# A hybrid decoder trunk on one core: the key norm by GpSimd powers, the triangular solve with every fourth column to a partition, and a beginning with x from ScalarE's queue

## The chip, the cores and the metric

The kernel runs on one core of a Trainium2 chip. The metric is the device time of one execution in microseconds, the median over runs. One core has TensorE (PE, matmuls and transposes), VectorE (DVE), ScalarE (ACT), GpSimd (POOL) and SyncE (SP, which issues DMAs here), each with an instruction queue of its own, and 16 DMA engines behind them.

## The reference

Two layers over 256 tokens of width 1024. Each layer has an FFN, a mixer of three branches (latent attention, gated linear attention, RWKV-7), cross-attention into 256 memory tokens and a second FFN, each between two RMS norms. All weights and results are float32.

```python
for l in range(DEPTH):                      # DEPTH = 2
    ng = norm_g[l]
    x = x + 0.5 * _rmsnorm(_swiglu(_rmsnorm(x, ng[0]), w_ffn_in[l, 0], w_ffn_out[l, 0]), ng[1])
    y = _mixer_block(_rmsnorm(x, ng[2]), ...)
    x = x + _rmsnorm(y, ng[3])
    y = _mem_attn(_rmsnorm(x, ng[4]), _rmsnorm(mem, mem_norm[l]), ...)
    x = x + _rmsnorm(y, ng[5])
    x = x + 0.5 * _rmsnorm(_swiglu(_rmsnorm(x, ng[6]), w_ffn_in[l, 1], w_ffn_out[l, 1]), ng[7])
```

The part of the RWKV branch that the change touches (8 heads of 64):

```python
kk = heads(k * k_k).astype(jnp.float32)
kk = kk / jnp.maximum(jnp.linalg.norm(kk, axis=-1, keepdims=True), 1e-12)
...
def step(state, inp):
    r_t, w_t, k_t, v_t, kk_t, a_t = inp
    sa = jnp.einsum('bhij,bhj->bhi', state, kk_t)
    state = (state * w_t[:, :, None, :] - sa[..., None] * (kk_t * a_t)[:, :, None, :]
             + v_t[..., None] * k_t[:, :, None, :])
    return state, jnp.einsum('bhij,bhj->bhi', state, r_t)
```

## The kernel before

**Order.** The kernel's body is recorded first, as a list of instructions with their tiles, and a list scheduler (class Program) gives each engine its order. It works out which instructions depend on which from the memory that they touch (`footprint`), estimates each one's duration (`cost`), knows that GpSimd and VectorE may share a port (`shared`), and simulates the queues (`forward`) in several passes. All instructions are issued from one line, L403, which is why every row of the profile names that line. Nothing is reordered later: each engine works through its list and waits at each instruction for what it needs. DMAs use eight completion semaphores in turn, in the order of issue, and each DMA waits until the one eight before it has landed.

**Products.** Activations and weights are split into two fp32r parts. `wload` brings a weight chunk into one of three raw buffers (raw0 to raw2); ScalarE casts it to `whi`, VectorE subtracts to `wlo`, and `mm3` makes three matmuls of each pair. Results are collected in the PSUM banks b_g0 and b_g1; transposes go through b_s0 and b_s1, and the branches use b_ya and b_yb. Most other data live in `heap` (float32) and `heapr` (fp32r), which the profile shows under one name each.

**Beginning.** While `fine` is set, the first FFN's weights come in pieces. x comes in four DMAs of 128x512 on SyncE's queue, the gain norm_g in two DMAs that broadcast 1024 values to 128 partitions. VectorE multiplies x by the gain, PE transposes the product into b_s, ScalarE casts it into heapr and VectorE subtracts for the low part. The mean square is applied behind the product.

**Key norm** (`rwkv_keys`). sv holds the squares of the keys, features on partitions. Four matmuls with `selh` sum them per head into 8 rows of 256 tokens (b_ya); VectorE takes a maximum into `rn`, ScalarE the square root, VectorE the reciprocal, and four matmuls with `wd` broadcast `rn` back to the 64 features of each head. VectorE then multiplies.

**Solve** (`rwkv_solve`, once for each layer and half of the tokens, four in all; t = 0 is called the first here, t = 1 the second). The recurrence over chunks of 32 tokens becomes the inverse of unit lower triangular 32x32 matrices. Of each matrix 4 partitions share the 32 columns, 8 each. VectorE does 31 steps of two instructions, multiply and subtract, on 128 x (31−j) x 8 elements. The result goes through DRAM twice, into `si` and `sx`, and is read back in other layouts as X1 and XT. In `rwkv_back` PE multiplies 32x32 blocks with X1; these are the `32x32` matmuls of the profile.

Of the kernel before, what the change touches and what calls it, by code (L numbers as in the profile page):

```python
# [24 lines left out]
D = 1024  # L25
# [23 lines left out]
class Program:  # L49
# [20 lines left out]
    def footprint(self, ap):  # L70
        t = ap.tensor
        if "PSUM" in str(ap.space):
            return [((ap.name, 0, 0), (1, 1))]
        if "DRAM" in str(ap.space):
            return [((ap.name, 0, 0), (1, 1))]
        key = (ap.name, ap.offset, ap.ap)
        f = self.prints.get(key)
        if f is None:
# [56 lines left out]
    def cost(self, op):  # L135
# [76 lines left out]
    def order(self):  # L212
# [10 lines left out]
        self.size = [o[2][0].nbytes() / self.DMA_RATE if o[0].name == "sync" else 0.0 for o in ops]  # L223
# [16 lines left out]
        for i, users in enumerate(self.users):  # L240
            t = self.at[i]
            for b in users:
                b.start, b.end = min(b.start, t[0]), max(b.end, t[1] + (4.0 if self.eng[i] == "sync" else 0.2))
        return order

    def lag(self, i, s):
        if self.eng[i] == "sync":
            return self.DMA_START + self.size[i] + self.DMA_END
        return self.LAT[self.eng[i]][self.eng[i] != self.eng[s]]
# [36 lines left out]
    def forward(self, rank):  # L286
# [15 lines left out]
        while len(order) < n:  # L302
# [9 lines left out]
            if e == "gpsimd" and t < held["vector"]:  # L312
                free[e] = held["vector"] + 0.03
                continue
# [3 lines left out]
            i = heapq.heappop(ready[e])[1]  # L318
            if e == "scalar" and self.table(ops[i]) not in (None, table):
# [58 lines left out]
            if e == "sync":  # L378
                dma_free = max(dma_free, t + self.DMA_START) + self.size[i]
                end = dma_free + self.DMA_END  # L380
                done.append(end)
            for s in self.succ[i]:
                rt[s] = max(rt[s], end if e == "sync" else end + self.LAT[e][e != eng[s]])
# [81 lines left out]
class Trunk:  # L465
# [184 lines left out]
    def constants(self):  # L650
# [38 lines left out]
        selh = self.tile("selh", [128, 134], F32)  # L689
        g.memset(selh, 0.0)  # L690
        g.memset(selh[0:64, 102:103], 1.0)
        g.memset(selh[64:128, 103:104], 1.0)
        self.selh = [selh[:, 6 - 2 * hp:134 - 2 * hp] for hp in range(4)]
        self.two = selh[:, 102:104]
# [12 lines left out]
        sel(e4.rearrange("p (a b) -> p a b", b=8), [[1, 32], [-1, 8]], 0, -8, op=ALU.is_equal)  # L707
# [37 lines left out]
        self.rn = self.tile("rn", [128, 256], F32)  # L745
        g.memset(self.rn, 0.0)
# [82 lines left out]
    def gain(self, src):  # L829
        b = self.h.alloc(D)  # L830
        for c in self.halves if self.fine else [slice(0, D)]:
            self.nc.sync.dma_start(b[:, c], src[c].partition_broadcast(128))
        return b

# [45 lines left out]
    def ffn(self, l, i, st, post_g, nxt, after_first=None):  # L880
        hb, lb, xh, xl = st["xp"]
        rs = st["rs"]
        wi = self.kview(self.w["w_ffn_in"][l, i])
# [7 lines left out]
        def inn(c):  # L891
# [14 lines left out]
            def view(k0, kn):  # L906
                return [(0, wi[:, k0:k0 + kn, c * 256:c * 256 + 256]), (256, wi[:, k0:k0 + kn, FF + c * 256:FF + c * 256 + 256])]
# [112 lines left out]
    def rwkv_keys(self, l):  # L1020
# [26 lines left out]
        for q in range(2):  # L1047
            pb = self.bank("ya", (2, 256))
            for j in range(2):
                hp = 2 * q + j  # L1050
                self.mm(pb[:, j, :], self.wd[:, hp * 128:hp * 128 + 128], self.rn)
                self.stt(kv[:, hp, :], k0[:, hp, :], self.col(l, 14 + hp), pb[:, j, :], MULT, MULT)
        for hp in range(4):
# [106 lines left out]
    def rwkv_solve(self, l, t):  # L1160
# [45 lines left out]
    def rwkv_back(self, l, t):  # L1206
# [9 lines left out]
        x1, hh = X1.v("p (h n) -> p h n", h=8), HH.v("p (h n) -> p h n", h=8)  # L1216
# [12 lines left out]
        h.free(X1, HH, LN)  # L1229
# [539 lines left out]
    def run(self):  # L1769
# [33 lines left out]
        nxt, st = into(0, 0)  # L1803
        self.fine = True
        for t in range(2):
            for c in self.halves:
                nc.sync.dma_start(self.x[:, t, c], w["x"][0, t * 128:t * 128 + 128, c])
        nxt(None)
        nxt(0)
        nxt(1)  # L1810
# [47 lines left out]
```

## Time and profile before

| | |
|---|---|
| median of 3 runs | 1641.55 us (1638.19 to 1644.56) |
| profiled execution | 1642.84 us, span 1641.1 us |
| mean granted TensorE clock | 0.99 |
| busy share of the span | PE 97%, VectorE 67%, ScalarE 59%, GpSimd 7% |
| bytes moved by DMA | 274.90 MB, mean 168 GB/s |

The table comes from the times and the page of the profiled execution. A row of the timeline gives start, length, engine, line, operation, tile written <- tiles read, shapes, count and, in brackets, the idle time ahead of it with what ended it. A row of the groups ends in busy time, mean ns of one, and idle time. A row of the chain of waits has start and length. A row of the DMA issues ends in the KB of one and the median us from issue to landing. A window's row has the busy time of each engine, then PE's granted clock, the share of the DMA engines and GB/s.

### The profile page before, as it was taken

The numbers are of one execution on the slowest core, as the hardware profiler recorded it, in microseconds if no ns is written. First come the engines' busy times: TensorE is split into PE (matmuls) and PEld (weight loads), VectorE is DVE, ScalarE is ACT, GpSimd is POOL, SyncE is SP. The second block draws the span as 40 slices with busy tenths as digits, with TensorE's granted clock in tenths as the row PEclk, the third lists the DMA queues.
The fourth block names the chain that finished last, engine by engine and source line by source line (L and its number), as shares of the span: only waits on it lengthen the run. The fifth ranks groups of instructions, "written<-read, shape, count | busy, mean of one in ns | idle before, by whom it ended". The sixth has DMA issues, their size and how long they took to land.

```text
span 1641.1 us, 23827 instructions
## 1 busy us (share of the span) xinstructions
PE 1591.3 (97%) x8623; PEld 1330.6 (81%) x8623; DVE 1102.5 (67%) x2110; ACT 967.3 (59%) x1889; POOL 113.2 (7%) x207
## 2 busy tenths in 40 slices
PE   7999999999999999999999999999999999999998
PEld 5788888877878987888878887987877889878886
DVE  5555668869967566555575556579699675675555
ACT  5455576769545556545565455858775565565554
POOL 7000010000200101000010001100002110010000
PEclk9999999999999999999999999999999999999999
DMA  7656543532656545555545555435337555354652
GB/s 247 224 167 203 164 153 96 173 91 92 229 159 199 193 142 166 201 197 188 196 158 193 192 185 156 142 97 167 98 98 229 181 184 188 114 189 160 207 178 103
DMA packets 206090, 274.90 MB, mean 168 GB/s; under 512 B 28148, under 2 KB 157650, under 8 KB 205972
## 3 DMA queue, kind: packets, MB, share of 16 engines
q1 hardware_dynamic: 205972, 273.39, 50.9%
q8 instruction: 67, 1.10, 0.3%
q14 instruction: 51, 0.42, 0.1%
HBM read 270.60 MB, written 2.75 MB: 167 GB/s over the span
## 4 chain that ended last, share of the span: by engine, by line
PE 79%; DVE 10%; ACT 5%; DMA 3%; issue 2%; SPq 0%; DVEq 0%; POOLq 0%; ACTq 0%; POOL 0%
PE b_g L403 42%; PE b_ya L403 15%; PE b_s L403 11%; PE b_yb L403 10%; DVE heap L403 5%; DVE wlo L403 3%; ACT heap L403 3%; DMA raw<-in_w_ffn_in_dram 1%; ACT whi L403 1%; DMA raw<-in_w_ffn_out_dram 1%; ACT L403 1%; DVE heapr L403 1%; DVE small L403 1%; DVE x L403 1%; DMA si<-heap 0%
## 5 line engine op out<-in xcount | busy, mean ns | idle before, releaser
L403 DVE TENSOR_TENSOR wlo<-raw,whi 128x512 fp32r<-128x512 f32 (+1 forms) x964 | 648.7, 688 | 382.7 <-ACT whi L403 370.8
L403 ACT CAST whi<-raw 128x512 fp32r<-128x512 f32 (+1 forms) x964 | 582.8, 620 | 457.1 <-PE b_g L403 218.3
L403 PE MATMUL b_g<-whi,heapr 128*128 128x512 f32 (+2 forms) x1904 | 651.7, 402 | 8.8 <-ACT heapr L403 6.0
L403 PEld LDWEIGHTS b_g<-whi,heapr 128*128 128x128 f32 x1904 | 356.9, 190 | 89.4 <-ACT heapr L403 10.2
L403 PE MATMUL b_g<-wlo,heapr 128*128 128x512 f32 (+2 forms) x952 | 365.3, 398 | 3.1 <-DVE wlo L403 3.1
L403 PEld LDWEIGHTS b_g<-wlo,heapr 128*128 128x128 f32 x952 | 180.6, 190 | 40.4 <-DVE wlo L403 5.9
L403 PE MATMUL b_g<-heapr,whi 128*128 128x256 f32 x1104 | 200.3, 291 | 1.7 <-DVE heap L403 1.5
L403 PE MATMUL b_ya<-whi,heapr 128*128 128x512 f32 x480 | 177.9, 394 | 0.3 <-ACT heapr L403 0.3
L403 PE MATMUL b_yb<-whi,heapr 128*128 128x512 f32 x480 | 175.6, 393 | 0.0
L403 PE MATMUL b_s<-whi,heapr 128*128 128x512 f32 x448 | 174.9, 399 | 0.0
L403 PEld LDWEIGHTS b_g<-heapr,whi 128*128 128x128 f32 x1104 | 165.0, 193 | 6.4 <-DVE heap L403 2.9
L403 DVE TENSOR_TENSOR heap<-heap 128x256 f32<-128x256 f32 (+29 forms) x376 | 130.9, 364 | 11.3 <-ACT heap L403 5.9
L403 PE MATMUL b_g<-heapr,wlo 128*128 128x256 f32 x552 | 131.8, 287 | 0.0
L403 POOL TENSOR_SCALAR small<-small 128x1 f32<-128x1 f32 (+2 forms) x52 | 34.3, 659 | 1276.2 <-ACT heap L403 1109.7
L403 PE MATMUL b_s<-ident,heap 128*128 128x128 f32 (+2 forms) x449 | 92.7, 276 | 13.0 <-DVE heap L403 10.4
L403 PEld LDWEIGHTS b_yb<-whi,heapr 128*128 128x128 f32 x480 | 89.8, 188 | 18.8 <-DVE heapr L403 0.2
L403 PEld LDWEIGHTS b_ya<-whi,heapr 128*128 128x128 f32 x480 | 89.3, 188 | 19.2 <-ACT heapr L403 0.5
L403 DVE TENSOR_TENSOR heapr<-b_s,heapr 128x256 fp32r<-128x256 f32 (+2 forms) x148 | 75.3, 510 | 37.6 <-ACT heapr L403 37.1
L403 ACT CAST heapr<-b_s 128x256 fp32r<-128x256 f32 (+2 forms) x148 | 65.4, 443 | 58.1 <-PE b_s L403 50.7
L403 PEld LDWEIGHTS b_s<-whi,heapr 128*128 128x128 f32 x448 | 83.6, 188 | 18.2 <-DVE heap L403 0.6
L403 PEld LDWEIGHTS b_g<-heapr,wlo 128*128 128x128 f32 x552 | 94.9, 192 | 0.6
L403 PE MATMUL b_ya<-wlo,heapr 128*128 128x512 f32 x240 | 92.9, 392 | 0.0
(161 smaller groups left out, 1540.7 us busy)
## 6 DMA issues: line engine op xcount, KB each, us to landing
raw<-in_w_ffn_in_dram SPq DMA_DIRECT2D x172, 512.0 KB, 4.9
raw<-in_w_in_dram SPq DMA_DIRECT2D x50, 1024.0 KB, 5.0
raw<-in_w_ffn_out_dram SPq DMA_DIRECT2D x44, 1024.0 KB, 6.9
raw<-in_mem_wkv_dram SPq DMA_DIRECT2D x16, 1024.0 KB, 5.4
raw<-in_w_branch_dram SPq DMA_DIRECT2D x12, 1024.0 KB, 5.4
raw<-in_w_out_dram SPq DMA_DIRECT2D x8, 1024.0 KB, 5.0
raw<-in_mem_wq_dram SPq DMA_DIRECT2D x8, 1024.0 KB, 5.2
raw<-in_mem_wo_dram SPq DMA_DIRECT2D x8, 1024.0 KB
```

Source lines behind the costliest of these rows:

```text
L403: getattr(eng.real, method)(*a, **k)
```

## The change

Five parts, all in one file:

1. *The scheduler.* A DMA issued by any engine is treated as one (before: only SyncE's). Inputs in DRAM make no dependencies, and other DRAM tensors make them by pieces of 32 elements. The rule for the port that VectorE and GpSimd share counts fewer GpSimd instructions. The whole order is planned anew.
2. *Weight loads.* While `fine` is set, the two halves of a piece of w_ffn_in come in one DMA: 8 of 128x2x256 stand where 16 of 128x256 stood.
3. *Key norm.* Eight matmuls of two columns give the sums with tokens on partitions (128 x 2 x 8); VectorE takes the maximum into `nz`, GpSimd raises it to the power −0.5, PE transposes `nz` twice, and ScalarE copies the result to the heap as rn. The broadcast matmuls stay. No Sqrt is left on ScalarE.
4. *Solve.* A partition holds every fourth column of its matrix. At step j only j//4 + 1 of the 8 columns are not zero yet, and only these are worked on. sx is written by four DMAs instead of one, and two ScalarE copies (XN) reorder X1 ahead of the 32x32 matmuls that read it.
5. *Beginning.* x and the gain come on ScalarE's queue, the gain as 8 rows of 128, which PE transposes to a column per block. x is transposed as it is, and VectorE multiplies by the gain while it reads PSUM.

Cut to what the prediction speaks of:

```diff
@@ cost, shared, forward
+        if method == "dma_start":
+            return 0.47
...
-        ins = [x for x in ins if int(np.prod(x.shape[1:])) > 1]
-        return len(ins) >= (2 if eng.name == "vector" else 1) or eng.name == "gpsimd"
+        if eng.name == "gpsimd":
+            return any(x is not k.get("scalar1", a[2] if len(a) > 2 else None) for x in ins)
+        return sum(int(np.prod(x.shape[1:])) > 1 for x in ins) > 1
@@ rwkv_keys
-        for hp in range(4):
-            self.mm(ps[:, 0:256], self.selh[hp], sv[:, hp, :], hp == 0, hp == 3)
-        rn = self.rn[96:104, :]
-        nc.vector.tensor_scalar(rn, ps[96:104, 0:256], 1e-24, None, MAX)
-        self.act(rn, rn, AF.Sqrt)
-        nc.vector.reciprocal(rn, rn)
+        for t in range(2):
+            for hp in range(4):
+                o = t * 8 + 2 * hp
+                self.mm(ps[:, o:o + 2], sv[:, hp, t * 128:t * 128 + 128], self.two)
+        nz = self.nz[:, :, 96:104]
+        nc.vector.tensor_scalar(nz, ps[:, 0:16].rearrange("p (t n) -> p t n", t=2), 1e-24, None, MAX)
+        nc.gpsimd.tensor_tensor(nz, nz, self.mhalf[:, 0:1].unsqueeze(1).to_broadcast([128, 2, 8]), ALU.pow)
+        pt = self.bank("ya")[:, 0:256]
+        for t in range(2):
+            self.tr(pt[:, t * 128:t * 128 + 128], self.nz[:, t, :])
+        rn = h.alloc(256)
+        nc.scalar.copy(rn.ap, pt)
@@ rwkv_solve
-            n = 31 - j
-            self.tt(tm[:, 0:n, :], xlv[:, j + 1:32, j:j + 1].to_broadcast([128, n, 8]),
-                    xx[:, j:j + 1, :].to_broadcast([128, n, 8]), MULT, eng)
-            self.tt(xx[:, j + 1:32, :], xx[:, j + 1:32, :], tm[:, 0:n, :], SUB, eng)
+            n, m = 31 - j, j // 4 + 1
+            self.tt(tm[:, 0:n, 0:m], xlv[:, j + 1:32, j:j + 1].to_broadcast([128, n, m]),
+                    xx[:, j:j + 1, 0:m].to_broadcast([128, n, m]), MULT, eng)
+            self.tt(xx[:, j + 1:32, 0:m], xx[:, j + 1:32, 0:m], tm[:, 0:n, 0:m], SUB, eng)
...
-        nc.sync.dma_start(sx, TM.ap)
+        sxw = sx.rearrange("(b a) (c x i) -> x b (a c) i", a=4, c=2, x=4)
+        for x in range(4):
+            nc.sync.dma_start(sxw[x], TM.v("p (c i) -> p c i", c=8)[x:128:4])
@@ rwkv_back
+        XN = h.alloc(256)
+        for b in (0, 64):
+            nc.scalar.copy(XN.v("p (h c x) -> p h c x", h=8, x=4)[b:b + 32], X1.v("p (h x c) -> p h c x", h=8, x=4)[b:b + 32])
@@ run, and new functions
+    def first_gain(self, src):
+        nc = self.nc
+        row, g = self.h.alloc(128), self.sm.alloc(8)
+        nc.scalar.dma_start(row[0:8, :], src.rearrange("(k c) -> k c", c=128))
+        ps = self.bank("ya")[:, 0:8]
+        self.tr(ps, row[0:8, :])
+        nc.vector.tensor_copy(g.ap, ps)
+        self.h.free(row)
+        return g
+
+    def first_norm(self, src, g, t, xh, xl, ss):
+        for hf, c in enumerate(self.halves):
+            ps = self.bank("s", (4, 128))
+            for j in range(4):
+                self.tr(ps[:, j, :], src[:, hf * 512 + j * 128:hf * 512 + j * 128 + 128])
+            xg = self.h.alloc(512)
+            xv, k = xg.v("p (k c) -> p k c", k=4), slice(hf * 4, hf * 4 + 4)
+            self.tt(xv, ps, g[:, k].unsqueeze(2).to_broadcast([128, 4, 128]), MULT)
+            self.split(xh[:, t, k, :], xl[:, t, k, :], xv)
+            self.h.free(xg)
+        jk = self.h.alloc(D)
+        self.meansq([src[:, c] for c in self.halves], jk, ss)
+        self.h.free(jk)
...
+        def load(t):
+            for c in self.halves:
+                nc.scalar.dma_start(self.x[:, t, c], w["x"][0, t * 128:t * 128 + 128, c])
+        load(0)
+        gb, pair, rs = self.first_gain(w["norm_g"][0, 0]), self.xpair(), [self.sm.alloc(2) for _ in range(2)]
+        load(1)
```

What the new plan makes of three places follows. In the changed file all instructions are issued from L415. The first place is ScalarE at the very beginning (`whi` is the cast of a weight piece, `heapr` that of the transposed x, ACTIVATE the square). Before:

```order
L403 ACT_TABLE_LOAD
L403 ACTIVATE heap_71,small_73<-x_74 128x512
L403 CAST whi0_78<-raw0_75 128x512
L403 CAST whi1_79<-raw0_75 128x512
L403 CAST heapr_72<-b_s0_69 128x512
L403 ACTIVATE heap_71,small_73<-x_74 128x512
```

After:

```order
L415 DMA x_74<-in_x_dram 128x512
L415 DMA heap_71<-in_norm_g_dram 8x128
L415 DMA x_74<-in_x_dram 128x512 x3
L415 ACT_TABLE_LOAD
L415 ACTIVATE heap_71,small_73<-x_74 128x512
L415 CAST whi0_78<-raw0_75 128x512
L415 CAST whi1_79<-raw0_75 128x512
L415 CAST heapr_72<-heap_71 128x512
```

Five DMA issues now stand ahead of the table load, the first square and the casts, and the cast into heapr reads the heap and no longer PSUM.

The second place is VectorE in the key norm of layer 0 (`rn` before, `nz` after, `wlo` the low parts of weights). Before:

```order
L403 TENSOR_SCALAR rn_122<-b_ya0_65 8x256
L403 TENSOR_TENSOR wlo2_88<-raw1_76,whi2_80 128x512
L403 TENSOR_TENSOR wlo4_90<-raw2_77,whi4_82 128x512
L403 SCALAR_TENSOR_TENSOR sgt_124<-b_s0_69,ocol_109,zt_119 32x128
L403 TENSOR_TENSOR heapr_72<-b_s1_70,heapr_72 128x384
L403 RECIPROCAL rn_122<-rn_122 8x256
```

After:

```order
L415 TENSOR_TENSOR heapr_72<-b_s0_69,heapr_72 128x384
L415 TENSOR_SCALAR nz_122<-b_ya1_66 128x2x8
L415 TENSOR_TENSOR heap_71<-heap_71 128x8x64 x2
L415 TENSOR_TENSOR wlo1_87<-raw1_76,whi1_79 128x512
L415 TENSOR_TENSOR wlo2_88<-raw1_76,whi2_80 128x512
L415 TENSOR_TENSOR wlo4_90<-raw2_77,whi4_82 128x512
```

The reciprocal is gone from VectorE's queue, and behind the maximum stand products and splits that read two tiles in SBUF. The power stands on GpSimd, and PE has 31 products between the last small matmul and the transposes of nz, and six more ahead of the broadcasts.

The third place is SyncE's queue behind the second solve of layer 0 (`si01` and `sx01` are the DRAM tiles of that solve, `heap` their source and target). Before:

```order
L403 DMA raw0_75<-in_w_branch_dram 128x4x512
L403 DMA si01_101<-heap_71 128x256
L403 DMA sx01_100<-heap_71 128x256
L403 DMA heap_71<-si01_101 32x32x8
L403 DMA heap_71<-sx01_100 32x8x32 x2
L403 DMA heap_71<-si01_101 32x32x8
L403 DMA heap_71<-sx01_100 32x8x32 x2
```

After:

```order
L415 DMA heap_71<-in_mem_norm_dram 128x1024
L415 DMA si01_101<-heap_71 128x256
L415 DMA sx01_100<-heap_71 256x1x32 x4
L415 DMA raw0_75<-in_w_in_dram 128x4x512
L415 DMA heap_71<-si01_101 32x32x8 x2
L415 DMA heap_71<-sx01_100 32x8x32 x4
```

Three more writes and a weight load of 1 MB now stand between the first write and the reads; the load of w_branch that stood ahead of the writes has moved away. On PE the 32x32 matmuls of the two solves of this layer stand some 15 us of PE work further forward than before.

More of the change, by code (lines that the diff above doesn't have):

```diff
@@ L73, in footprint @@
             return [((ap.name, 0, 0), (1, 1))]
-        if "DRAM" in str(ap.space):
-            return [((ap.name, 0, 0), (1, 1))]
+        if ap.name.startswith("in_"):
+            return []
         key = (ap.name, ap.offset, ap.ap)
         f = self.prints.get(key)
+        if f is None and "DRAM" in str(ap.space):
+            idx = np.array([ap.offset])
+            for st, n in ap.ap:
+                if st:
+                    idx = (idx[:, None] + st * np.arange(n)[None, :]).reshape(-1)
+            f = self.prints[key] = [((ap.name, 0, pg), (1, 1)) for pg in np.unique(idx // 32).tolist()]
         if f is None:
@@ L222, in order @@
                 self.succ[j].append(i)
-        self.size = [o[2][0].nbytes() / self.DMA_RATE if o[0].name == "sync" else 0.0 for o in ops]
+        self.dma = [o[1] == "dma_start" for o in ops]
+        self.size = [o[2][0].nbytes() / self.DMA_RATE if d else 0.0 for o, d in zip(ops, self.dma)]
         self.cols = [self.columns(o) if o[0].name == "tensor" else 0.0 for o in ops]
@@ L242, in order @@
             for b in users:
-                b.start, b.end = min(b.start, t[0]), max(b.end, t[1] + (4.0 if self.eng[i] == "sync" else 0.2))
+                b.start, b.end = min(b.start, t[0]), max(b.end, t[1] + (4.0 if self.dma[i] else 0.2))
         return order
     def lag(self, i, s):
-        if self.eng[i] == "sync":
+        if self.dma[i]:
             return self.DMA_START + self.size[i] + self.DMA_END
@@ L311, in forward @@
             t, e = best
-            if e == "gpsimd" and t < held["vector"]:
-                free[e] = held["vector"] + 0.03
-                continue
             while wait[e] and wait[e][0][0] <= t:
@@ L318, in forward @@
             i = heapq.heappop(ready[e])[1]
+            if e == "gpsimd" and self.port[i] and t < held["vector"]:
+                heapq.heappush(ready[e], (rank[i], i))
+                free[e] = held["vector"] + 0.03
+                continue
             if e == "scalar" and self.table(ops[i]) not in (None, table):
@@ L377, in forward @@
             end = t + c
-            if e == "sync":
+            if self.dma[i]:
                 dma_free = max(dma_free, t + self.DMA_START) + self.size[i]
                 end = dma_free + self.DMA_END
-                done.append(end)
+                if e == "sync":
+                    done.append(end)
             for s in self.succ[i]:
-                rt[s] = max(rt[s], end if e == "sync" else end + self.LAT[e][e != eng[s]])
+                rt[s] = max(rt[s], end if self.dma[i] else end + self.LAT[e][e != eng[s]])
                 left[s] -= 1
@@ L553, in wload @@
     def wload(self, loads, heads=False):
+        both = None
+        if not isinstance(loads, list):
+            both, loads = loads, [(g * loads.shape[3], loads[:, :, g, :]) for g in range(2)]
         k = loads[0][1].shape[1]
@@ L561, in wload @@
             kk = slice(j, j + 1) if self.fine else slice(0, k)
+            if self.fine and both is not None:
+                self.nc.sync.dma_start(rv[:, j, :].rearrange("p (g n) -> p g n", g=2), both[:, j])
+                continue
             for off, v in loads:
@@ L687, in constants @@
             sel(self.mask[p0:p0 + 64, 64:128], [[1, 64]], 0, -1)
[L689 to L694, printed above, removed]
+        self.two = self.tile("two", [128, 2], F32)
+        g.memset(self.two, 0.0)
+        g.memset(self.two[0:64, 0:1], 1.0)
+        g.memset(self.two[64:128, 1:2], 1.0)
         self.wd = self.tile("wd", [128, 512], F32)
@@ L744, in constants @@
         sel(self.ag[32:64, :], [[0, 256]], 16, -1)
-        self.rn = self.tile("rn", [128, 256], F32)
-        g.memset(self.rn, 0.0)
+        self.nz = self.tile("nz", [128, 2, 128], F32)
+        g.memset(self.nz, 0.0)
         self.xa = self.tile("xa", [128, 256], F32)
@@ L830, in gain @@
         b = self.h.alloc(D)
-        for c in self.halves if self.fine else [slice(0, D)]:
-            self.nc.sync.dma_start(b[:, c], src[c].partition_broadcast(128))
-        return b
+        self.nc.sync.dma_start(b.ap, src.partition_broadcast(128))
+        return b
+    def first_gain(self, src):
[20 more added lines that the diff above has]
+        self.h.free(jk)
     def meansq(self, halves, jk, ss, over=1):
@@ L1801, in late @@
             self.rope_tables()
-        nxt, st = into(0, 0)
         self.fine = True
-        for t in range(2):
[L1806 to L1810, printed above, removed]
+        def load(t):
[4 more added lines that the diff above has]
+        load(1)
+        for t in range(2):
+            self.first_norm(self.x[:, t, :], gb, t, pair[2], pair[3], rs[t])
+        self.sm.free(gb)
+        st = dict(xp=pair, rs=rs)
         for l in range(DEPTH):
```

15 lines of the change are left out of this document (8 added, 7 removed).

## The prediction, made before the changed kernel ran

> **What bounds the kernel now.** I read the busy table and the chain of waits first, then the windows, then the timeline and the groups at the three changed places.
>
> ```profile
> PE 1591.3 (97%) x8623; PEld 1330.6 (81%) x8623; DVE 1102.5 (67%) x2110; ACT 967.3 (59%) x1889; POOL 113.2 (7%) x207
> PE 79%; DVE 10%; ACT 5%; DMA 3%; issue 2%; SPq 0%; DVEq 0%; POOLq 0%; ACTq 0%; POOL 0%
> 0.00:40.00 40.00, 28.77 (x121) 22.06 (x122) 23.16 (x38) 23.18 (x44) 31.06 (x101) 1.00 0.79 245
> 262.75:266.16 3.41, 3.39 (x12) 3.04 (x13) 2.26 (x6) 2.24 (x4) 0.00 (x0) 0.50 0.95 284
> 464.14:470.97 6.83, 6.83 (x75) 5.57 (x75) 0.69 (x1) 2.52 (x6) 0.00 (x0) 0.50 0.88 295
> 1075.12:1078.53 3.41, 3.41 (x15) 3.22 (x14) 2.60 (x7) 0.47 (x1) 0.00 (x0) 0.50 0.97 303
> 1273.10:1279.92 6.82, 6.82 (x55) 5.68 (x54) 1.38 (x2) 4.04 (x10) 0.00 (x0) 0.50 0.73 243
> ```
>
> TensorE (PE) is busy 97% and holds 79% of the chain. The matmuls of the big products stay, so a change elsewhere can only win PE's idle time and stretches at half speed. The windows' columns are start and end, length, busy time of PE, PE's weight loads, VectorE, ScalarE and GpSimd, PE's granted clock, the DMA share and GB/s. The first 40 us leave PE idle for 11.2. The other four windows are stretches at clock 0.50, found just behind the key norms (3.41 us each) and the second solve of each layer (6.83). PE loses half of each there: 1.7 behind a key norm, 3.4 behind a solve.
>
> **The beginning.**
>
> ```profile
> heap<-in_norm_g_dram SPq DMA_DIRECT2D x2, 256.0 KB
> 4.72 0.78 DVE L403 TENSOR_TENSOR heap<-x,heap 128x512 f32<-128x512 f32 x1 [4.72 <-DMA heap<-in_norm_g_dram]
> 5.65 1.09 PE L403 MATMUL b_s<-ident,heap 128*128 128x128 f32 x4 [5.65 <-DVE heap L403]
> 8.63 0.79 PE L403 MATMUL b_g<-whi,heapr 128*128 128x512 f32 x1 [1.90 <-ACT heapr L403]
> 15.35 0.63 ACT L403 ACTIVATE heap<-x 128x512 f32<-128x512 f32 x1 [0.84 <-DMA x<-in_x_dram]
> 16.60 0.50 PE L403 MATMUL b_g<-whi,heapr 128*128 128x512 f32 x1 [1.63 <-ACT heapr L403]
> 37.85 0.44 PE L403 MATMUL b_s<-ident,heap 128*128 128x128 f32 x2 [2.05 <-DVE heapr L403]
> ```
>
> The first product starts at 8.63. It waited for the gain rows (4.72), the transposes (5.65) and the cast. Now x is transposed raw, so PE no longer waits for the gains; VectorE multiplies while it empties PSUM, then ScalarE casts and VectorE takes the difference. That is one more link behind the transposes, 0.78 by the row at 4.72, against a start that no longer waits for gains until 4.72. Ahead of its first cast ScalarE now issues five DMAs, and the last of them waits until the first piece of x has landed, with the table load, the square and the weight casts queued behind it. So I expect the first product within a microsecond of 8.63. The gain is what follows: x's second half is no longer behind weight pieces (1.63 at 16.60), and 512 KB of broadcast gains are not moved, 2.1 us at 245 GB/s. Not all of this reaches PE, since the third weight buffer and the first loads behind it feed the rest. The 2.05 at 37.85 is untouched. The weight pieces of the first two buffers become eight DMAs where sixteen stood; that saves issues on SyncE, whose queue (SPq) holds 0% of the chain: nothing. I take −2, the bytes alone. The ends are −4 (both the 1.63 and the 2.1) and +2.5, if ScalarE's queued work starts later by the 0.84 us that it waited for x at 15.35 and by two such links of 0.78.
>
> The Trainium skill (page "DMA: Bandwidth & Descriptors", section "Issuing engines are not separate DMA queues") says that DMAs issued from several engines run on the same 16 DMA engines, interleaved, and that only issuing time is saved. By it a queue of its own does not bring x sooner through the weights, and the 1.63 stays; without it the term would be −3.7 and the time 1631. The DMA share of 0.79 in the first 40 us speaks for the page as far as it goes.
>
> **The key norm.**
>
> ```profile
> 253.27 1.89 PE L403 MATMUL b_ya<-heap,selh 128*128 128x256 f32 x8
> 256.52 0.43 DVE L403 TENSOR_SCALAR rn<-b_ya 8x256 f32<-8x256 f32 x1
> 256.80 1.28 ACT L403 ACT_TABLE_LOAD   x1
> 258.10 0.41 ACT L403 ACTIVATE rn<-rn 8x256 f32<-8x256 f32 x1
> 259.12 1.75 DVE L403 RECIPROCAL rn<-rn 8x256 f32<-8x256 f32 x1
> 261.02 1.10 PE L403 MATMUL b_ya<-rn,wd 128*128 128x256 f32 x4 [2.04 <-DVE rn L403]
> 262.77 1.22 PE L403 MATMUL b_ya<-rn,wd 128*128 128x256 f32 x2 [0.65 <-DVE heap L403]
> 1072.89 1.13 PE L403 MATMUL b_ya<-rn,wd 128*128 128x256 f32 x4 [2.31 <-DVE rn L403]
> 1074.73 0.88 PE L403 MATMUL b_ya<-rn,wd 128*128 128x256 f32 x2 [0.71 <-DVE heap L403]
> 269.23 1.17 PE L403 MATMUL b_ya<-rkb,heap 128*128 128x2 f32 x10
> L403 POOL TENSOR_TENSOR small<-small,mhalf 128x1 f32<-128x1 f32 x44 | 33.3, 760 | 3.3
> L403 POOL TENSOR_TENSOR small<-small,mhalf 128x4 f32<-128x4 f32 x4 | 4.5, 1122 | 0.3
> L403 POOL TENSOR_TENSOR small<-small,mhalf 128x8 f32<-128x8 f32 x4 | 6.9, 1724 | 0.3
> 419.74 3.52 POOL L403 TENSOR_SCALAR small<-small 128x4 f32<-128x4 f32 x1 [65.68 <-DVE small L403]
> 1242.39 0.20 POOL L403 TENSOR_SCALAR small<-small 128x4 f32<-128x4 f32 x1 [4.79 <-DVE small L403]
> ```
>
> PE now waits 2.04 + 0.65 in layer 0 and 2.31 + 0.71 in layer 1; with 1.7 of half clock behind each that is 9.1 us. The chain from the maximum to the broadcast takes 261.02 − 256.52 = 4.5 us.
>
> After: eight matmuls of two columns cost 8 × 0.23 = 1.9 (a float32 matmul leaves two records, so ten are five in 1.17), as much as the four removed (1.89); two transposes add about 0.5 per layer. The power runs over 16 columns. From 4 to 8 columns it grew by 0.60 us, 0.15 a column, so 16 take 1.72 + 8 × 0.15 = 2.9. The maximum (0.43 at most), 2.9, the transposes, a ScalarE copy (about 0.4, as the Sqrt over as many columns) and the hops make 4.5 to 5: no shorter than now. What PE has beside it also stays level, but it is dealt otherwise: 31 products, about 4 us, cover the maximum and the power, six more the copy. In calm this leaves some tenths; I take 1 us of gap per layer, and a half clock behind every second one (0.85): 2 × 1.85 = 3.7. With the transposes, B = 3.7 + 1.0 − 9.1 = −4.4. The best is −8.1, no gap at all. The worst is a power kept waiting: the 128x4 TENSOR_SCALAR of 0.20 took 3.52 amid VectorE's two-input work, so 3.3 more per layer, with the half clock of both as now: 2 × (3.3 + 1.0 + 1.7) + 1.0 − 9.1 = +4. The two table loads saved per layer (1.28 each) lie on ScalarE, which is 59% busy; I count nothing, for PE's other work covers them.
>
> The Trainium skill (page "SBUF — State Buffer", section "Who interferes with whom") says that a VectorE instruction with two SBUF inputs and a GpSimd one that reads SBUF exclude each other for the whole instruction. The trace agrees (0.20 against 3.52). By that rule alone, with VectorE's products and splits queued right behind the maximum, the key norm would gain nothing.
>
> **The solve.**
>
> ```profile
> 376.00:440.00 64.00, 60.96 (x319) 50.06 (x318) 61.22 (x142) 48.53 (x79) 8.58 (x6) 1.00 0.41 142
> 377.29 0.41 DVE L403 TENSOR_TENSOR heap<-heap 128x248 f32<-128x248 f32 x1
> 1262.58 0.16 DVE L403 TENSOR_TENSOR heap<-heap 128x8 f32<-128x8 f32 x1
> 453.37 7.86 DMA si<-heap
> 461.65 2.02 DMA heap<-sx
> 463.81 1.29 PE L403 MATMUL b_ya<-heap 32*32 32x32 f32 x32 [2.30 <-DMA heap<-sx]
> 1266.65 5.18 DMA heap<-sx
> 1271.97 0.78 PE L403 MATMUL b_ya<-heap 32*32 32x32 f32 x32 [1.40 <-DMA heap<-sx]
> sl<-heap SPq DMA_DIRECT2D x16, 32.0 KB, 4.3
> heap<-sx SPq DMA_DIRECT2D x16, 32.0 KB, 2.1
> 1272.75 0.75 ACT L403 COPY heap<-b_ya 32x256 f32<-32x256 f32 x2 [1.91 <-PE b_ya L403]
> ```
>
> A step goes from 0.41 at 248 elements to 0.16 at 8, so 1.04 ns an element. A solve has 2 × 3968 elements now and 2 × 1560 afterwards: 4816 × 1.04 = 5.0 us less VectorE in each of four, 20 in all. VectorE is 96% busy in the window of the second solve (61.22 of 64), so the solve ends earlier. But PE's wait is for the round trip through DRAM behind it: 2.30 and 1.40, with 3.41 of half clock each, 10.5 us in two places; the two first solves cost nothing. The write of sx becomes four pieces of 32 KB in runs of 128 bytes; each lands after 2.1 to 4.3 us by the two nearest rows, so up to 2.2 later, and issuing three more costs SyncE something. Two copies of 0.37 are added ahead of the 32x32 matmuls, but X1 comes before XT and the DMA wait covers them; without that cover they cost 0.75 a solve. If all else stood, the matmuls would be ready 5.0 − 2.2 − about 1 = 1.8 earlier, near the 1.40 and below the 2.30. All else does not stand: the new order takes these matmuls forward, by some 15 us of PE work at both solves of a layer, as VectorE has as much less work ahead of its last step. So the waits are drawn anew at four places. I take 1 us of gap at each and the 3.4 at one in three: 4 × (1 + 1.1) = 8.5 against 10.5, −2. The ends: −10.5 (no wait), and +12 (all four like the 2.30 + 3.4 now: 22.8 − 10.5).
>
> **The rest of the order** is planned anew with the same products; 0, as some stalls move. **Sum**: −2 − 4.4 − 2 = −8.4 from the profiled execution's 1642.8 (1.7 of it outside the span), so 1634.4. It lies 1.3 above the median of the runs, 1641.55; on that scale 1633.
>
> **Rivals.**
> - The solves become the new wait (slower). The round trip is four writes, then reads, with the matmuls 15 us further forward; at the second solve of layer 0 SyncE's queue now also holds a 1 MB load of w_in between writes and reads, 3.5 us at the 295 GB/s of the window at 464.14. At a gap of 4 us in each of the four places, with its half clock, C is 4 × 7.4 − 10.5 = +19, and the time 1633 + 2 + 19 = 1654. It decides from a gap of about 3 on. For it: 5.18 for one read of sx. Against: VectorE's 96% and 5 us less on it.
> - The power is locked out by VectorE, as in the row of 3.52: B is 0 to +4, 1637 to 1641; no measurable change.
> - One of the two waits vanishes wholly: the solve's (−10.5) gives 1624.7, the key norm's (−8.1) 1629.4; 1627 between them. For it: the chains lie within about 2 us of their cover.
> - The beginning gives nothing or loses 2.5, because ScalarE is held by its fourth load of x: 1635 to 1637.5.
>
> **How the numbers follow.** Forecast 0.42 (own range 1628 to 1638), solves 0.12, lock 0.13, a wait vanishing 0.23, beginning 0.10. About 0.5% (8.2 us) is what a measurement of this kernel can tell from no change; faster than that is below 1633.3. That takes in the whole of the vanishing waits and some six tenths of the forecast's: 0.48. Slower is the solves' case, 0.12; the rest, 0.40, is the same. The range goes from 1622 to 1646, which leaves out most of the slower case and the best sums.
>
> **What would show it.** Beginning: PE's first product near 8.6, no 1.63 at its tenth. Key norm: the power over 128x16 at 2.9 and not 6; the wait ahead of the rn broadcasts about 1, and clock 1.00 behind it. Solve: steps of 128x31 near 0.18, VectorE's total some 20 us lower, and the waits ahead of the 32x32 matmuls about 1 at all four. What would make me wrong: those waits at 3 or more with a clock of 0.50 behind them, a power of 5 us, or new idle time of PE at places that I priced at nothing.

## The result, and the profile after

The changed kernel takes 1631.15 us (median of 4 runs, 1630.45 to 1633.05) against 1640.78 before (4 runs, 1638.19 to 1644.56). The ratio is 0.9937, 95% interval [0.9923, 0.9951]: faster by 0.6%, some 10 us. The profiled execution took 1633.05 us with a span of 1631.3, against 1642.84 and 1641.1 before: 9.8 less.

The page's busy table and its chain of waits:

```profile
PE 1587.8 (97%) x8644; PEld 1327.7 (81%) x8644; DVE 1085.2 (67%) x2109; ACT 962.8 (59%) x1891; POOL 116.3 (7%) x209
PE 79%; DVE 11%; ACT 4%; DMA 2%; issue 2%; SPq 1%; POOL 0%; DVEq 0%; ACTq 0%
```

VectorE has 17.3 us less to do (1102.5 before), yet PE's share is the same 97%. Where the time went is read first from two landmarks, the transposes with which each layer's mixer begins. Two rows of the timeline before, two of after:

```profile
207.07 0.65 PE L403 MATMUL b_s<-ident,heap 128*128 128x128 f32 x4 [2.38 <-DVE heap L403]
1016.66 0.75 PE L403 MATMUL b_s<-ident,heap 128*128 128x128 f32 x4 [2.38 <-DVE heap L403]
```

```profile
203.55 0.66 PE L415 MATMUL b_s<-ident,heap 128*128 128x128 f32 x4 [2.35 <-DVE heap L415]
1010.75 0.66 PE L415 MATMUL b_s<-ident,heap 128*128 128x128 f32 x4 [2.38 <-DVE heap L415]
```

Up to the first mixer 3.5 us are won, from there to the second 2.4 (807.2 against 809.6), behind it 3.9 (620.6 against 624.4).

**Beginning.** The same timeline rows as in the prediction, after:

```profile
4.02 1.08 PE L415 MATMUL b_s<-ident,x 128*128 128x128 f32 x4 [4.02 <-POOL heap L415]
5.54 0.69 DVE L415 TENSOR_TENSOR heap<-b_s,small 128x512 f32<-128x512 f32 x1
7.88 0.80 PE L415 MATMUL b_g<-whi,heapr 128*128 128x512 f32 x1 [0.76 <-ACT heapr L415]
14.07 0.66 PE L415 MATMUL b_s<-ident,x 128*128 128x128 f32 x4 [1.02 <-DVE heap L415]
34.64 0.44 PE L415 MATMUL b_s<-ident,heap 128*128 128x128 f32 x2 [0.77 <-DVE heapr L415]
37.02 0.49 PE L415 MATMUL b_s<-whi,heapr 128*128 128x512 f32 x1 [0.53 <-DVE heap L415]
```

The first product starts 0.75 us sooner, the wait of 1.63 is gone with one of 1.02 ahead of later transposes of x in its place, and the 2.05 at 37.85 has become 0.77 + 0.53.

**Key norm.** GpSimd's two powers, VectorE's work beside the first of them, and PE's transposes and broadcasts in layer 0:

```profile
252.58 3.29 POOL L415 TENSOR_TENSOR nz<-nz,mhalf 128x16 f32<-128x16 f32 x1 [23.46 <-DVE nz L415]
1059.08 2.91 POOL L415 TENSOR_TENSOR nz<-nz,mhalf 128x16 f32<-128x16 f32 x1 [9.34 <-DVE nz L415]
253.65 1.88 DVE L415 TENSOR_TENSOR wlo<-raw,whi 128x512 fp32r<-128x512 f32 x3
255.93 0.44 PE L415 MATMUL b_ya<-ident,nz 128*128 128x128 f32 x2
256.92 1.04 PE L415 MATMUL b_ya<-heap,wd 128*128 128x256 f32 x4
```

No bracket stands behind PE's rows: it waits for neither. The three splits of VectorE, each with two tiles in SBUF as inputs, lie wholly inside the power and took 0.68 us each, against a mean of 0.69 over the run, so VectorE was not held up by the power here. The window 252 to 262 has clock 1.00 and PE busy for 9.89 of 10 us:

```profile
252.00:262.00 10.00, 9.89 (x75) 9.18 (x75) 9.81 (x24) 6.87 (x16) 4.25 (x2) 1.00 0.41 122
```

**Solve.** The second solve of each layer, PE and (for layer 0) SyncE's reads, then the first solves of layer 0 and of layer 1 on ScalarE and PE, then the stretches at half clock:

```profile
436.74 4.54 SPq L415 DMA_DIRECT2D heap<-sx  x4
442.22 1.14 PE L415 MATMUL b_ya<-heap 32*32 32x32 f32 x32 [2.92 <-DMA heap<-sx]
1246.42 1.30 PE L415 MATMUL b_ya<-heap 32*32 32x32 f32 x32 [1.94 <-DMA heap<-sx]
316.21 0.64 ACT L415 COPY heap<-heap 32x256 f32<-32x256 f32 x1 [1.32 <-DMA heap<-si]
317.70 0.64 PE L415 MATMUL b_yb<-ident,heap 128*96 128x128 f32 x4 [1.29 <-ACT heap L415]
319.95 1.16 PE L415 MATMUL b_yb<-heap 96*128 96x128 f32 x8 [0.58 <-ACT heap L415]
1132.07 1.35 ACT L415 COPY heap<-heap 32x256 f32<-32x256 f32 x2 [1.39 <-DMA heap<-si]
1134.91 0.66 PE L415 MATMUL b_s<-heap 128*64 128x128 f32 x8 [1.68 <-ACT heap L415]
1136.70 0.85 PE L415 MATMUL b_ya<-heap 32*32 32x32 f32 x32 [0.41 <-DMA heap<-sx]
441.36:448.18 6.82, 5.96 (x76) 4.92 (x77) 1.38 (x2) 3.56 (x8) 0.00 (x0) 0.50 0.73 243
1137.68:1144.50 6.82, 6.82 (x56) 5.82 (x55) 1.32 (x2) 2.97 (x8) 0.00 (x0) 0.50 0.01 2
1246.90:1253.73 6.83, 6.83 (x79) 5.76 (x76) 1.39 (x2) 3.54 (x9) 0.00 (x0) 0.50 0.72 238
```

Both old waits are still there, 2.92 and 1.94, and new ones have come at the first solves: in layer 1 ScalarE's copy into XN waits 1.39 us for the read of si, and PE then 1.68 for what stands behind the copy on ScalarE; in layer 0 the copy waits 1.32 and PE 1.29 and 0.58. Three stretches of 6.8 us at half clock follow where there were two.

### The profile page after: what moved, and what is told of

It is laid out like the page before. It is cut to its first block, busy times and chain, and to the rows that moved or that the text cites. A ratio compares the mean times of both kernels' runs of the same rounds, so it can differ in the third digit from the quotient of the medians.

```text
span 1631.3 us, 23864 instructions
## 1 busy us (share of the span) xinstructions
PE 1587.8 (97%) x8644; PEld 1327.7 (81%) x8644; DVE 1085.2 (67%) x2109; ACT 962.8 (59%) x1891; POOL 116.3 (7%) x209
## 4 chain that ended last, share of the span: by engine, by line
PE 79%; DVE 11%; ACT 4%; DMA 2%; issue 2%; SPq 1%; POOL 0%; DVEq 0%; ACTq 0%
PE b_g L415 42%; PE b_ya L415 15%; PE b_s L415 12%; PE b_yb L415 10%; DVE heap L415 6%; DVE wlo L415 3%; ACT heap L415 2%; ACT whi L415 1%; DMA heap<-sx 1%; DMA heap<-sl 1%; DMA raw<-in_w_ffn_in_dram 1%; DVE zq L415 1%; SPq L415 1%; DVE x L415 1%; DVE heapr L415 0%
## 5 line engine op out<-in xcount | busy, mean ns | idle before, releaser
L415 DVE TENSOR_TENSOR wlo<-raw,whi 128x512 fp32r<-128x512 f32 (+1 forms) x964 | 648.2, 688 | 385.3 <-ACT whi L415 378.8
L415 ACT CAST whi<-raw 128x512 fp32r<-128x512 f32 (+1 forms) x964 | 583.6, 620 | 456.2 <-PE b_g L415 224.3
L415 PE MATMUL b_g<-whi,heapr 128*128 128x512 f32 (+2 forms) x1904 | 653.9, 404 | 4.5 <-ACT heapr L415 2.9
L415 PEld LDWEIGHTS b_g<-whi,heapr 128*128 128x128 f32 x1904 | 356.8, 190 | 85.4 <-ACT heapr L415 6.7
L415 PE MATMUL b_g<-wlo,heapr 128*128 128x512 f32 (+2 forms) x952 | 368.9, 402 | 2.2 <-DVE wlo L415 2.2
L415 PEld LDWEIGHTS b_g<-wlo,heapr 128*128 128x128 f32 x952 | 180.6, 190 | 38.7 <-DVE wlo L415 3.4
L415 PE MATMUL b_g<-heapr,whi 128*128 128x256 f32 x1104 | 199.0, 288 | 1.7 <-DVE heap L415 1.0
L415 PE MATMUL b_ya<-whi,heapr 128*128 128x512 f32 x480 | 177.2, 394 | 0.0
L415 PE MATMUL b_yb<-whi,heapr 128*128 128x512 f32 x480 | 176.3, 393 | 0.0
L415 PE MATMUL b_s<-whi,heapr 128*128 128x512 f32 x448 | 175.4, 399 | 0.5 <-DVE heap L415 0.5
L415 PEld LDWEIGHTS b_g<-heapr,whi 128*128 128x128 f32 x1104 | 163.1, 191 | 5.9 <-DVE heap L415 2.1
L415 PE MATMUL b_g<-heapr,wlo 128*128 128x256 f32 x552 | 132.1, 289 | 0.0
L415 DVE TENSOR_TENSOR heap<-heap 128x256 f32<-128x256 f32 (+24 forms) x376 | 112.8, 315 | 12.6 <-ACT heap L415 4.9
L415 POOL TENSOR_SCALAR small<-small 128x1 f32<-128x1 f32 (+2 forms) x52 | 28.2, 543 | 1275.1 <-ACT heap L415 1112.4
L415 PEld LDWEIGHTS b_yb<-whi,heapr 128*128 128x128 f32 x480 | 89.8, 188 | 18.6 <-DVE heapr L415 0.2
L415 PEld LDWEIGHTS b_ya<-whi,heapr 128*128 128x128 f32 x480 | 89.3, 188 | 18.7 <-ACT heap L415 0.2
L415 ACT CAST heapr<-b_s 128x256 fp32r<-128x256 f32 (+2 forms) x144 | 63.0, 439 | 64.2 <-PE b_s L415 56.9
L415 PEld LDWEIGHTS b_s<-whi,heapr 128*128 128x128 f32 x448 | 83.8, 188 | 19.5 <-DVE heap L415 1.6
L415 PE MATMUL b_s<-ident,heap 128*128 128x128 f32 x433 | 91.7, 276 | 5.5 <-DVE heap L415 4.7
L415 PEld LDWEIGHTS b_g<-heapr,wlo 128*128 128x128 f32 x552 | 93.8, 191 | 1.6 <-issue 0.5
L415 DVE TENSOR_TENSOR heapr<-b_s,heapr 128x256 fp32r<-128x256 f32 (+2 forms) x144 | 72.6, 505 | 32.3 <-ACT heapr L415 31.9
L415 PE MATMUL b_ya<-wlo,heapr 128*128 128x512 f32 x240 | 93.0, 392 | 0.0
```

The lines of the kernel that those rows point to most:

```text
L415: getattr(eng.real, method)(*a, **k)
```

## The experiments

All were timed in five rounds beside the kernel before; ratios are to before. The first four do one part of the change alone.

**Key norm alone** (the hunks of `rwkv_keys` and its constants).

> The kernel before with the key norm of the change alone; scheduler, solve and beginning as before. Theory 1 (the gain is the key norm's own: power, transposes and copy lie under PE's products, so both gaps of 2.0 to 2.3 us, the 0.7 behind them and the half clock go): 9.1 less about 1 for the transposes, -8 us, ratio 0.995, and no wait ahead of the rn broadcasts. Rival (only the new plan, with its other rule for the shared port, keeps VectorE's two-input work away from the power): with the old rule the power over 16 columns takes 4 us or more instead of 2.9, the gaps stay over 1.5 and the time is within 2 us of before.

Measured: 1637.57 us, ratio 0.9967 [0.9955, 0.9979], 5.4 us faster. The power took 3.29 us and 3.33 under the old rule, and the gaps are gone but for 0.81 in layer 1. The rival falls. The 8 us are not reached: other waits came up, such as this one of the timeline, at a place where 1.5 us were lost before:

```profile
381.35 0.50 PE L403 MATMUL b_g<-whi,heapr 128*128 128x512 f32 x1 [1.98 <-ACT heap L403]
```

**Beginning alone** (`first_gain`, `first_norm`, `run`, the joined weight loads, and of the scheduler's new rules the one that knows ScalarE's DMAs as DMAs).

> The kernel before with the new beginning alone (x and gains on ScalarE's queue, raw transposes, joined weight pieces; DMAs of ScalarE known to the scheduler as DMAs, nothing else of its rules). Theory 1: the 3.6 us less idle PE in the first 200 us of the changed kernel are the beginning's own: -3.5 us, ratio 0.998, first product at 7.9. Rival (they come from the other rules of the plan, or are given back behind it): within 1 us of before.

Measured: 1634.21 us, ratio 0.9949 [0.9936, 0.9961], 8.4 us faster. The first mixer begins here:

```profile
202.95 0.65 PE L407 MATMUL b_s<-ident,heap 128*128 128x128 f32 x4 [2.35 <-DVE heap L407]
```

That is 4.1 us before 207.07. The rest is won behind it, in an order that this kernel also has planned anew; the expectation was too low, and by what the rest is won isn't shown.

**Solve alone** (`rwkv_solve`, the XN copies of `rwkv_back` and the starting columns).

> The kernel before with the new solve alone. Theory 1 (PE waits for the round trip through DRAM, which the change does not shorten, and the planner moves the 32x32 matmuls forward by what VectorE saves): between -3 and +6 us, waits of 1.5 us or more with half clock at two or more of the four solves, though VectorE has some 20 us less to do. Rival (VectorE's relief reaches PE): -5 us or better, and the waits of 2.30 and 1.40 gone.

Measured: 1642.58 us, ratio 0.9998 [0.9987, 1.0008]. VectorE is busy for 1085.0 us instead of 1102.5, and nothing comes of it. Of the details only a part came true: no 32x32 matmul has a wait, but PE waits 2.14 us at 458.21, behind VectorE, and 1.27 at 333.99 and 1.26 at 1148.10, both behind ScalarE, whose copy into XN had waited for si, 0.67 us at the first place and 2.89 at the second:

```profile
1146.42 0.66 ACT L403 COPY heap<-heap 32x256 f32<-32x256 f32 x1 [2.89 <-DMA heap<-si]
```

**Scheduler rules alone** (the hunks of class Program).

> The kernel before with the new scheduler rules alone, the same instructions in another order. Theory 1 (re-planning moves stalls, it does not remove them): within 3 us of before, the waits at the key norm still there. Rival (the plan is what gains): -5 us or better.

Measured: 1640.43 us, ratio 0.9986 [0.9976, 0.9997]. The wait at the key norm of layer 1 became longer, 3.40 us. Theory 1 holds. The four parts alone give 5.4 + 8.4 + 0.3 + 2.3 = 16.4 us by their ratios, together they give 10.3: they do not add.

The next three leave one part out of the changed kernel.

**Without the new solve** (the hunks of "solve alone" taken back).

> The changed kernel with the old solve (8 adjacent columns to a partition, all 8 worked on, one write of sx, no XN); the rest changed, order planned anew. Theory 1 (the solve's part brings nothing, its waits are drawn anew by the plan): within 3 us of the changed kernel, ratio to before 0.993 to 0.996. Rival (VectorE's 20 us less are part of the gain): 5 us or more slower than the changed kernel, ratio 0.997 or more.

Measured: 1634.19 us, ratio 0.9957 [0.9943, 0.9972], 3.3 us behind the changed kernel by the ratios, and the intervals overlap. VectorE has its old load (1101.1 us). Closer to theory 1 than to the rival, but not told apart from a small gain of the solve.

**Without the new key norm** (those of "key norm alone" taken back).

> The changed kernel with the old key norm; the rest changed, order planned anew. Theory 1 (the key norm's gaps and half clock come back, 9 us, less what was given back elsewhere when the norm alone gained 5): 5 to 8 us slower than the changed kernel, ratio to before 0.997 to 0.998, waits of 1.5 us or more ahead of the rn broadcasts. Rival (parts replace each other: beginning with new DMA rules alone gave 8 already): within 2 us of the changed kernel.

Measured: 1636.97 us, ratio 0.9969 [0.9955, 0.9983], 5.3 us behind the changed kernel. The wait came back in layer 0; in layer 1 the broadcasts found their rn in time in this order. The time is as theory 1 has it.

```profile
259.55 1.10 PE L415 MATMUL b_ya<-rn,wd 128*128 128x256 f32 x4 [1.87 <-DVE rn L415]
```

**Without the new scheduler rules** (footprint, shared port and the wait for it taken back).

> Key norm, solve and beginning of the change under the old rules of the scheduler (only DMAs of ScalarE are known to it as DMAs). Theory 1 (the rules only deal the stalls anew): within 3 us of the changed kernel, ratio to before 0.992 to 0.996. Rival (the rules carry part of the gain): 4 us or more slower than the changed kernel.

Measured: 1630.32 us, ratio 0.9925 [0.9912, 0.9937], within the interval of the changed kernel. A gain of the rules does not show. In this order PE waits 1.53 us for ScalarE's copy of rn at the key norm of layer 0, which it does not in the changed kernel.

The last five keep the changed kernel's order and replace instructions one for one (`instead` issues another call at the place of the one before it).

**All 8 columns again, in the same order.**

```diff
+            nc.instead((tm[:, 0:n, :], xlv[:, j + 1:32, j:j + 1].to_broadcast([128, n, 8]),
+                        xx[:, j:j + 1, :].to_broadcast([128, n, 8]), MULT))
...
+            nc.instead((xx[:, j + 1:32, :], xx[:, j + 1:32, :], tm[:, 0:n, :], SUB))
```

> The changed kernel in its own order, instruction for instruction, but each step of the solve works on all 8 columns as before: 4816 elements more per solve, 5 us of VectorE each, 20 in all. Theory 1 (what VectorE saves there does reach the end of the solve, and the plan has spent it by moving the 32x32 matmuls forward): waits ahead of the 32x32 matmuls grow by 3 to 5 us at the four solves, +10 to +18 us on the changed kernel, ratio to before 1.000 to 1.005. Rival (VectorE is not on the path of these waits): within 2 us of the changed kernel.

Measured: 1651.72 us, ratio 1.0064 [1.005, 1.0077], some 20.8 us slower than the changed kernel; VectorE is busy for 1103.2 us, 18.0 more. So VectorE's saving is on the path, all of it and a little more. But not where I expected it: the waits ahead of the 32x32 matmuls grew from 2.92 to 3.13 and from 1.94 to 2.31, and the time went at products that wait for VectorE's other work, queued among the steps:

```profile
304.17 1.09 PE L419 MATMUL b_yb<-ident,heap 128*96 128x128 f32 x4 [4.05 <-DVE heap L419]
388.58 1.22 PE L419 MATMUL b_yb<-trig,heap 128*128 128x128 f32 x4 [2.82 <-DVE heap L419]
1202.07 0.71 PE L419 MATMUL b_yb<-trig,heap 128*128 128x128 f32 x4 [2.62 <-DVE heap L419]
```

As I read it, the plan has spent VectorE's 18 us: it moved PE's instructions forward until they just fit.

**Reads that need no write.**

```diff
+            nc.instead((xt[32 * q:32 * q + 32, :, 32 * q:32 * q + 32],
+                        self.ix.rearrange("(q h a) (c i) -> q (a c) h i", q=4, h=8, c=8)[q]))
```

(and the same for X1.)

> The changed kernel in its own order, but the reads behind the solve take the same bytes in the same runs from another DRAM tile that was written long before, so they wait for no write of si or sx (the values are not the solve's). Theory 1 (the round trip through DRAM is what ends last at the solves): the waits of 2.92 and 1.94 us ahead of the 32x32 matmuls go, with the half clock of 6.83 us behind each and a third one at the first solve of layer 1: -6 to -12 us on the changed kernel, ratio to before 0.986 to 0.990. Rival (the wait is only passed on, to VectorE or ScalarE behind it): within 2 us of the changed kernel.

Measured: 1629.98 us, ratio 0.9932 [0.9917, 0.9947], the same as the changed kernel, and the wait is still there:

```profile
435.77 6.58 SPq L419 DMA_DIRECT2D heap<-ix  x6
442.49 0.22 PE L419 MATMUL b_ya<-heap 32*32 32x32 f32 x2 [2.88 <-DMA heap<-ix]
```

My theory of the round trip fell: the reads are late although nothing has to be written for them. Six issues take 6.58 us. In both kernels the third read behind the weight load is the long one, 3.0 us in the changed kernel and 3.2 here, where most others take about half a microsecond. For the changed kernel's four reads of sx the view of the tile shows it (shortest, median and longest in ns, then first and last start):

```profile
L415 SPq DMA_DIRECT2D heap<-sx x4: 445/460/3038, 436.7 to 440.8; - x4
```

In SyncE's queue a 1 MB load stands just ahead of them.

**The weight load behind the reads**, one move in SyncE's queue at each solve. The queue's order at the second solve of layer 0:

```diff
 DMA sx01_100<-heap_71 256x1x32 x4
-DMA raw0_75<-in_w_in_dram 128x4x512
 DMA heap_71<-si01_101 32x32x8 x2
 DMA heap_71<-sx01_100 32x8x32 x4
+DMA raw0_75<-in_w_in_dram 128x4x512
```

> The changed kernel in its own order, but at each of the four solves the one 1 MB weight load that stood in SyncE's queue between the writes and the last reads now stands behind the last read. Theory 1b (in place of the one that fell: the reads do not wait for their data but SyncE's issue of the third read behind that load, 3.0 and 3.1 us where 0.45 is usual, since the load's pieces fill the DMA queues first): no issue over 1 us there, waits ahead of the 32x32 matmuls of the second solves under 0.5 us, no half clock behind them, -6 to -11 us on the changed kernel, ratio to before 0.987 to 0.990, the best of all. Rival (the four writes in runs of 128 bytes block the queues): the long issues stay or move to another read, within 2 us of the changed kernel.

Measured: 1628.23 us, ratio 0.9918 [0.9905, 0.9932], the best of those that leave nothing out, though its interval and that of the changed kernel overlap. It is 3.1 us faster than the changed kernel by the ratios, where 6 to 11 were expected. The mechanism is as expected: four reads are issued in 1.90 us instead of 4.54, and the 32x32 matmuls do not wait.

```profile
434.34 1.90 SPq L438 DMA_DIRECT2D heap<-sx  x4
437.60 0.69 PE L438 MATMUL b_ya<-heap 32*32 32x32 f32 x30 [0.16 <-DMA heap<-sx]
446.65 0.63 ACT L438 ACTIVATE heap<-heap 128x512 f32<-128x512 f32 x1 [4.23 <-DMA heap<-in_mem_dram]
447.89 1.16 PE L438 MATMUL b_ya<-heap 64*128 64x128 f32 x14 [2.70 <-ACT heap L438]
```

The price was not. The load of the memory tokens (in_mem) now lands behind two weight loads; ScalarE waits 4.23 us for it with a copy that PE needs queued behind, and PE waits 2.70 ten microseconds later than before, and 2.87 likewise in layer 1. A wait removed from a queue came back in the next.

**One write of sx.**

```diff
+            nc.instead(*([(sx, TM.ap)] if x == 0 else []))
```

> The changed kernel in its own order, but sx is written by one DMA of 128 rows of 1 KB, as before, in place of four in runs of 128 bytes (the columns then lie in another order, so the values are not the solve's). Theory 1b (the load between writes and reads is what holds the reads): the reads follow some 1.9 us earlier in the queue, but the third read is held until the load has gone, so waits at the second solves shrink by 2 us at most, with the half clock of one of them; 0 to -5 us on the changed kernel. Rival (the four writes are the cause): both waits gone, -8 us or better.

Measured: 1621.81 us, ratio 0.9879 [0.9863, 0.9895], 9.5 us faster than the changed kernel by the ratios. Its values are not the solve's, so this is no kernel to use; it shows what the four writes cost. Neither forecast is right. The waits at the second solves stay (theory 1b), 2.07 and 2.11 us, with reads issued in 4.89:

```profile
430.20 4.89 SPq L419 DMA_DIRECT2D heap<-sx  x4
435.17 0.22 PE L419 MATMUL b_ya<-heap 32*32 32x32 f32 x2 [2.07 <-DMA heap<-sx]
310.96 0.68 ACT L419 COPY heap<-heap 32x256 f32<-32x256 f32 x1
```

Yet the four writes cost more than I gave them (the rival's price), at the first solves. SyncE issues them in 2.5 us ahead of the reads of si, for which ScalarE's copies into XN wait. With one write the copy at 310.96 waits for nothing, where the one of the changed kernel waited 1.32 and PE behind it 1.29 and 0.58; and the 1.68 + 0.41 at the first solve of layer 1 are gone with the half clock behind them (3.4). That makes 6.9 us after 0.44 that stays. At the second solve of layer 0 0.85 us of wait and half of a 3.41 stretch go, together 9.5 in all, less 0.7 at the last solve. This list comes from one profiled execution of each kernel. They differ by 11.2, of which 1.2 stands already at the first mixer (202.31 against 203.55), ahead of anything that the edit touches.

**x from SyncE's queue.**

```diff
+            if method == "dma_start":
+                eng = self.sync
             getattr(eng.real, method)(*a, **k)
```

> The changed kernel in its own order, but the five DMAs of x and the gain are issued by SyncE, between the weight loads where the plan's time puts them. Theory 1 (what gains at the beginning is raw x and the small gain, not the queue): the first product between 7.5 and 8.5, the mixer of layer 0 reached within 1 us of the changed kernel's 203.6, time within 2 us of it. Rival (ScalarE's queue is what brings x sooner): the mixer 2 us or more later, up to before's 207.

Measured: 1629.75 us, ratio 0.9927 [0.9915, 0.9939]. The first product starts at 8.30, the mixer at 203.19, against 203.55. Theory 1 holds: x's later pieces arrive later (2.72 of wait at 7.75 where ScalarE's queue had 0.92 at 6.23), and nothing of it is left at the mixer. A single profile tells no more than about 1 us there: the four runs before this one have the changed kernel's beginning, instruction for instruction, and reach the mixer between 202.31 and 203.10.

```profile
7.75 0.90 PE L420 MATMUL b_s<-ident,x 128*128 128x128 f32 x3 [2.72 <-DMA x<-in_x_dram]
8.30 0.78 PE L420 MATMUL b_g<-whi,heapr 128*128 128x512 f32 x1
203.19 0.66 PE L420 MATMUL b_s<-ident,heap 128*128 128x128 f32 x4 [2.35 <-DVE heap L420]
```

The Trainium skill (page "DMA: Bandwidth & Descriptors", section "Issuing engines are not separate DMA queues") says that only issuing time is saved by several issuers; this pair of runs agrees: the mixer comes 0.4 us sooner from SyncE's queue, less than that spread.

## Why the prediction was right, and its terms were not

The direction and the time (1633 against 1631.15) were right, and so was the mechanism at two of three places. The sizes were not, and errors cancelled.

- *The beginning*, −2: measured 3.5 at the first mixer, and up to 4.8 in the runs that share this beginning (203.55 down to 202.31, against 207.07). The step "the 2.05 at 37.85 is untouched" failed; it became 0.77 + 0.53, and in two of those runs no wait over 0.4 us is left there. The first product's start (within 1 us of 8.63) held, and so did the view that the queue brings nothing. That the bytes alone bring the gain is not shown: the smaller gain, the raw transposes and the joined weight loads were not separated.
- *The key norm*, −4.4: in its place all 9.1 us went, 5.7 of waits and 3.4 of half clock. The mis-sized step is "1 us of gap per layer, and a half clock behind every second one"; the gap was 0. It depends on the order: with the key norm alone 0.81 was left in layer 1, without the new rules 1.53 in layer 0. The power's 2.9 was right (2.91 and 3.29). The lock's rival is out: the power ran beside a VectorE that was busy 9.81 of 10 us, and its two times lie 0.4 apart. The Trainium skill (page "SBUF — State Buffer", section "Who interferes with whom") lets the one that issues first hold the shared port; these runs show neither a power nor the 0.68 us splits beside it held up, so its rule did not decide here. The row of 3.52 stays unexplained by them. As a part of the whole it is worth 5.3 to 5.4 (alone, and left out), since other waits come up.
- *The solve*, −2: in its places it lost. The waits listed above are 2.92 + 1.94 + 1.68 + 0.41 in place of 2.30 + 1.40, with 1.29 + 0.58 at the first solve of layer 0: 8.8 against 3.7; a third stretch at half clock adds 3.4. That is +8.5. At the first solves the step that failed is "X1 comes before XT and the DMA wait covers them". It looked at PE alone. ScalarE's copy waits at the head of its queue, and what PE needs stands behind it; one write of sx in place of four showed it. At the second solves it is "PE's wait is for the round trip through DRAM behind it", carried over to the changed kernel: the 2.92 stayed 2.88 where nothing had to come back, and went to 0.16 where the weight load, and with it the issue of 3.0 us, was out of the way. My rival for the slower side named the right objects, the four writes and the 1 MB load; each of its waits stayed below the 3 us from which it decides.
- *The rest of the order*, 0: these three places sum to −3.7 − 9.1 + 8.5 = −4.3 (with the waits of the beginning at 3.7). The other waits of over 0.4 us and half clocks changed by +0.3. The profiled executions differ by 9.8. So 5.8 us lie in no wait that I can name; PE's busy time is 3.5 lower although half clock took 1.7 more. One group of matmuls, the same 256 in both kernels, holds 3.8 of it. The groups by shape before and after, and two rows of the changed kernel's timeline:

```profile
L403 PE MATMUL b_ya<-heap 64*128 64x128 f32 x256 | 28.6, 288 | 0.5 <-ACT heap L403 0.3 <-DVE heap L403 0.2
L415 PE MATMUL b_ya<-heap 64*128 64x128 f32 x256 | 24.8, 286 | 0.0
269.18 2.20 PE L415 MATMUL b_ya<-heap 64*128 64x128 f32 x16
451.47 1.16 PE L415 MATMUL b_ya<-heap 64*128 64x128 f32 x16
```

  One of them takes the same 0.29 us on average. But sixteen take 2.20 us where they start one by one, some 0.11 us apart, and 1.16 where they start in pairs, 0.01 us apart, and the changed kernel has 73 such pairs where 42 stood. Some 2 us stay open; runs of one kernel differ by 2.6 (after) to 6.4 us (before).

That the whole is near the sum is therefore in part luck: the terms erred by −2, −5, +10 and −6. The key norm is supported by leaving it out (5.3) and by itself (5.4), the beginning only by itself (8.4, of which 4.1 in its place), and the rules of the scheduler and the solve are each within 3.3 us of nothing.

## What to carry to other kernels

A small copy that waits for a DMA is not covered by another engine's wait: look at what stands behind it in its own queue, and who waits for that. Where a planner orders the work, time saved on an engine beside the bound can be spent at once on moving instructions forward, as it seems to have been here, so that the saving shows up neither as idle time nor as speed; keep the order fixed and undo the saving to see what it carries. And a wait must be named by its queue before it is treated: a read that "waits for a write" waited for its own issue.

## What the runs showed of the hardware that I had not expected

- A read issued third behind a 1 MB load, with two reads of 32-byte runs between, took 3.0 to 3.4 us to issue at both second solves of the five kernels that keep the changed kernel's order there, and 0.42 to 0.47 where the load stood behind it. At the first solves of the changed kernel, where the load stood between the reads of si and those of sx, no read took over 0.7 to issue. Whether the load's pieces or the reads of si fill the queue was not told apart.
- A power of 2.91 to 3.29 us on GpSimd ran beside VectorE instructions with two SBUF inputs, 0.68 us each as elsewhere.
- VectorE's time has no fixed price beside a busy PE: 17.5 us less of it gave 0.3 us where the order was planned anew, and 18.0 us more cost 20.8 where the order was kept.
